# The banks of the latent queries' other products, a later rotation, and row maxima that begin 14 groups behind the gate keys

## The chip, the cores and the metric

The kernel runs on one core of one Trainium2 chip. The metric is the time of one execution on the device in microseconds (us). The kernel before was timed three times; the median stands for it. One further execution was recorded by the hardware profiler, and every row of a profile below comes from that one.

## The reference, cut to what matters

Two layers over a sequence of 1024 tokens with 1024 features. Each layer projects the normalized input once and gives parts of it to three mixers: retention (4 heads), latent attention (8 heads, "mla") and gated linear attention (4 heads, "gla"). Their gated outputs are joined and projected back.

```python
for l in range(DEPTH):                                   # DEPTH = 2
    h = rms_norm(x, norm_w[l]) * (1 + scale) + shift     # scale, shift, gate from c @ ada_w[l]
    ret_p, mla_p, gla_p = split_cols(h @ w_in[l], ...)
    rq, rk, rv, rz = split_cols(ret_p, RET_SPLIT)
    r_o = rms_norm(retention(rope(rq), rope(rk), rv))
    mq, mkv, mkr, mz = split_cols(mla_p, MLA_SPLIT)
    m_o = mla(mq, mkv, mkr, ...)
    gq, gk, gv, gg, gz = split_cols(gla_p, GLA_SPLIT)
    g_o = rms_norm(gla(gq, gk, gv, gg, ...), gla_norm[l])
    x = x + gate * (concat(r_o * silu(rz), m_o * silu(mz), g_o * silu(gz)) @ w_out[l])

def mla(q_lat, kv_lat, k_rope, ...):
    q = rms_norm(q_lat) @ w_uq                # per head 64 plain and 32 rotated columns
    q_nope, q_pe = q[..., :64], rope(q[..., 64:], pos)
    k_nope, v = split(rms_norm(kv_lat) @ w_ukv);  k_pe = rope(k_rope)
    sc = (q_nope . k_nope + q_pe . k_pe) * scale, masked by chunk
    return softmax(sc) @ v
```

## The kernel before, in words

Products are taken in single precision from operands that are split in a high and a low part, so that each product is a group of three matmuls (`mm3`, L556 to L558: high by high, high by low, low by high). TensorE (PE) runs its instructions in the order in which the program writes them. The queues of the other engines, SyncE's (SP) among them, which issues the transfers, are put in order by a scheduler. The accumulators lie in four pools of two banks each: `pj`, `mm`, `s` and `acc`. A product may begin in a bank when the instructions that read the bank's last product are done.

Small pieces of work run beside the large projections. `task(steps, wait)` registers a generator, `tick()` stands behind each group of three matmuls and counts the waits down, a generator's `yield n` puts it off for n groups, and `drain` runs a task out.

The stages of a layer around the change, in the order of TensorE, with their names in the tiles of the profile:

- `mla_queries`, first part: four products of the rotated query columns. They are copied to tiles `mq_qx`, two for each half of the sequence. The first half is rotated there and then (`q_rope`).
- `rz0`: the first half of retention's gate, `proj_silu` (copy from the bank L717, silu in L430 to L435 on ScalarE, VectorE and GpSimd).
- `mla_queries`, the rest: eight products p0 to p7 of the plain query columns (four pairs of heads `pr`, two halves `hf` of the sequence). Each has two groups (0.23 us a matmul), and each is read by ScalarE (cast to the high part `mq_ph`, L1108) and by VectorE (low part `mq_pl`, L1109), and goes to memory (`qn`, L1111). Behind p7 `q_rope` rotates the second half: six products on VectorE (`rope_half`, L732 to L737; the tiles `mrope_ra` and `mrope_rb` hold two of them, the rest is done in place in `mq_qx`), two casts on VectorE (`mrope_qrh`, L1120), two subtractions on GpSimd (`mrope_qrl`, L1121), four transfers to memory (`qr`, L1123).
- `rz1`: the second half of retention's gate, as `rz0`.
- `gk`: the gate keys, 16 groups of three. Beside them run `head_out` (L874 on TensorE, L878 on VectorE: it multiplies retention's output by the gate, then L883 writes it to memory, `md`) and the first row maxima, `mla_max`.
- `gv`, and then the gate stages of the other mixers.

`ret_core` runs beside all of these stages up to the end of `rz1`. Per chunk pair and head group it makes scores (L790), masks them on VectorE (`retc_ram`, L793), takes the state products (L815, states `mq_rst` L825), and sums the output in a bank of `acc` (L830, L834, with `retc_rqs` of GpSimd, L798); ScalarE copies it out (`retc_ho`, L850) and squares it (L860), VectorE sums the squares (`hnorm`, L862), and GpSimd normalizes (L864).

`mla_max` finds the maximum of each row of raw scores before the attention. `load(h)` brings the rows of head h to one of two pairs of tiles: `mmax_mxk` (keys) and `mmax_mxq` (queries: plain rows from `qn` L1149, rotated rows from `qr` L1151, both halves of the sequence at once). Twelve matmuls per head (L1244) each with a maximum on VectorE (L1246) follow, one about every 1.45 groups, and the results are put together behind them (L1213 to L1220). `wgk`, `wgv` and `wgz` are weights: their high part is cast by ScalarE (L456), the low part is subtracted by GpSimd (L457). `ada_aw` (L575 loads, L576 on VectorE) prepares the modulation of layer 1 during layer 0. `glap_wg` (L891) is a small weight read for the decay (matmul L908).

Of the kernel before, what the change touches and what calls it, by code (L numbers as in the profile page):

```python
# [162 lines left out]
class Builder:  # L163
# [903 lines left out]
    def mla_queries(self, l, ql, tab):  # L1067

        nc = self.nc
        w, wn = self.weight((l, "uq"))  # L1070
        self.lab = "mq_"
        x = [[], []]
        for hf in range(2):
            for i in range(2):
                ps = self.ps("pj")
                self.uq_mtile(w, ql, i, hf, ps)
                x[hf].append(self.pt(name="qx"))
                nc.scalar.copy(x[hf][i], ps)
            if hf == 0:
                self.q_rope(l, x[hf], hf, *tab[hf])  # L1080
                self.lab = "mq_"
        yield
        self.lab = "mq_"
        for pr in range(4):
            for hf in range(2):
                ps = self.ps("pj")
                self.uq_mtile(wn, ql, pr, hf, ps)
                self.pair_out(self.qn[l], pr, hf, ps)
        self.q_rope(l, x[1], 1, *tab[1])

    def mla_keys(self, l, kvl):
# [376 lines left out]
    def layer(self, l, src):  # L1468
        nc = self.nc
        self.chunks.extend([(l, 4), (l, 5)] + ([(l + 1, i) for i in (0, 2, 1, 3)] if l + 1 < DEPTH else []))  # L1470
        mixed = [None] * 8
# [30 lines left out]
        queries = self.mla_queries(l, ql, tab)  # L1502
        next(queries)
        mixed[0] = self.proj_silu(l, "rz0")
        self.next_chunk("f")
        next(queries, None)
        mixed[1] = self.proj_silu(l, "rz1")
        self.drain(core)
        self.next_chunk("g")
        big = self.task(self.mla_max(l), 8)  # L1510
        hout = self.task(self.head_out(l, ro, mixed, (0, 1)))
        gk = self.proj_halves(l, "gk", float(GDK ** -0.5))
        self.drain(hout)
# [75 lines left out]
```

## Time and profile before

| what | value |
|---|---|
| median of 3 runs | 1170.69 us (1167.6, 1170.69, 1170.9) |
| the profiled execution | 1170.77 us, its span 1169.0 us |
| mean granted TensorE clock | 0.984 of full speed |
| TensorE busy | 1117.3 us, 96% of the span, 5968 matmuls |
| VectorE busy | 792.6 us, 68% |
| ScalarE busy | 596.0 us, 51% |
| GpSimd busy | 527.0 us, 45% |
| transfers | 169.01 MB, mean 145 GB/s |

The span is what the trace covers; some 1.8 us of the execution lie outside it. Busy shares are means over stages that differ, so what the change is worth is read in the stages that it touches. In a row of a timeline stand the start in us, the duration in us, engine, line, operation, and output<-input; "x2" says that two such instructions in a row are taken together; a bracket gives the idle time of the engine just before and what ended it. Layer 0 passes the stages around the change about 562.7 us earlier than layer 1.

### The profile page before, as it was taken

The numbers are of one execution on the slowest core, as the hardware profiler recorded it, in microseconds if no ns is written. First come the engines' busy times: TensorE is split into PE (matmuls) and PEld (weight loads), VectorE is DVE, ScalarE is ACT, GpSimd is POOL, SyncE is SP. The second block draws the span as 40 slices with busy tenths as digits, with TensorE's granted clock in tenths as the row PEclk, the third lists the DMA queues.
The fourth block names the chain that finished last, engine by engine and source line by source line (L and its number), as shares of the span: only waits on it lengthen the run. The fifth ranks groups of instructions, "written<-read, shape, count | busy, mean of one in ns | idle before, by whom it ended". The sixth has DMA issues, their size and how long they took to land.

```text
span 1169.0 us, 16968 instructions
## 1 busy us (share of the span) xinstructions
PE 1117.3 (96%) x5968; PEld 937.6 (80%) x5968; DVE 792.6 (68%) x1366; ACT 596.0 (51%) x1164; POOL 527.0 (45%) x459
## 2 busy tenths in 40 slices
PE   6999999999999899999999999989999989999996
PEld 4778987788877788887887898778888778888896
DVE  7866585688777366768875467674876735686754
ACT  6434343433544678853543434434355467886421
POOL 0064144444533456773565333534552344668620
PEclk8999999999999999999999999999999989999998
DMA  9816563561146534248443356255212653424722
GB/s 372 298 53 181 186 225 109 188 203 41 42 136 179 132 91 109 64 158 301 171 171 103 111 172 239 77 190 160 64 41 64 178 132 91 109 64 168 255 82 73
DMA packets 65585, 169.01 MB, mean 145 GB/s; under 512 B 10262, under 2 KB 13334, under 8 KB 65500
## 3 DMA queue, kind: packets, MB, share of 16 engines
q1 hardware_dynamic: 65500, 167.93, 45.4%
q8 instruction: 47, 0.77, 0.3%
q14 instruction: 38, 0.31, 0.1%
HBM read 125.36 MB, written 38.41 MB: 140 GB/s over the span
## 4 chain that ended last, share of the span: by engine, by line
PE 74%; DVE 12%; DMA 5%; ACT 4%; issue 4%; POOL 1%; SPq 0%; DVEq 0%; ACTq 0%; POOLq 0%
PE mhead_psacc L1295 3%; PE mhead_psacc L1293 3%; PE mhead_psacc L1294 3%; PE pmz_pspj L556 3%; PE pmz_pspj L557 2%; PE pmz_pspj L558 2%; DMA ada_aw<-awc 2%; PE wo_pspj L558 2%; PE wo_pspj L556 2%; PE wo_pspj L557 2%; PE wo_pss L558 2%; PE wo_pss L556 2%; PE wo_pss L557 2%; PE mhead_pss L1262 2%; PE mhead_pss L1261 2%
## 5 line engine op out<-in xcount | busy, mean ns | idle before, releaser
L457 POOL TENSOR_TENSOR wwo_wl<-wwo_wst,wwo_wh 128x1024 fp32r<-128x1024 f32 x27 | 69.3, 2570 | 40.8 <-ACT wwo_wh L456 33.7
L1270 POOL TENSOR_TENSOR mhead_wh<-mhead_p,mhead_wh 128x384 fp32r<-128x384 f32 (+1 forms) x48 | 58.1, 1210 | 46.2 <-DVE mhead_wh L1269 46.2
L576 DVE SCALAR_TENSOR_TENSOR ada_aw<-ada_aw,silrow 128x512 f32<-128x512 f32 x64 | 60.6, 966 | 20.7 <-DMA ada_aw<-awc 20.7
L1246 DVE TENSOR_REDUCE mmax_mx<-mmax_psmm 128x1 f32<-128x512 f32 (+1 forms) x96 | 57.4, 598 | 25.0 <-PE mmax_psmm L1244 23.5
L1275 DVE TENSOR_TENSOR mhead_ph<-mhead_pss,mhead_ph 128x512 fp32r<-128x512 f32 x48 | 33.0, 688 | 41.9 <-ACT mhead_pss L1274 41.9
L556 PE MATMUL pmz_pspj<-mkh_h,wmz_wh 128*128 128x512 f32 x128 | 53.6, 418 | 0.0
L557 PE MATMUL pmz_pspj<-mkh_h,wmz_wh 128*128 128x512 f32 x128 | 50.9, 397 | 0.0
L558 PE MATMUL pmz_pspj<-mkh_h,wmz_wl 128*128 128x512 f32 x128 | 50.7, 396 | 0.0
L1270 POOL TENSOR_TENSOR mhead_wl<-mhead_p,mhead_wl 128x128 fp32r<-128x128 f32 (+1 forms) x48 | 35.8, 747 | 32.7 <-DVE mhead_wl L1269 32.7
L558 PE MATMUL wo_pspj<-gran_mx,wwo_wl 128*128 128x512 f32 (+1 forms) x120 | 45.1, 375 | 1.9 <-POOL wwo_wl L457 1.9
L556 PE MATMUL wo_pspj<-gran_mx,wwo_wh 128*128 128x512 f32 (+1 forms) x120 | 45.2, 377 | 0.3 <-ACT wwo_wh L456 0.3
L557 PE MATMUL wo_pspj<-gran_mx,wwo_wh 128*128 128x512 f32 (+1 forms) x120 | 44.7, 372 | 0.0
L556 PE MATMUL wo_pss<-gran_mx,wwo_wh 128*128 128x512 f32 (+1 forms) x120 | 44.6, 372 | 0.0
L558 PE MATMUL wo_pss<-gran_mx,wwo_wl 128*128 128x512 f32 (+1 forms) x120 | 44.2, 368 | 0.0
L557 PE MATMUL wo_pss<-gran_mx,wwo_wh 128*128 128x512 f32 (+1 forms) x120 | 44.2, 368 | 0.0
L600 ACT ACTIVATE ssq_sq<-ssq_x 128x512 f32<-128x512 f32 (+1 forms) x31 | 16.6, 534 | 52.0 <-DVE ssq_x L1372 52.0
L457 POOL TENSOR_TENSOR wrk_wl<-wrk_wst,wrk_wh 128x1024 fp32r<-128x1024 f32 x3 | 8.0, 2676 | 75.7 <-ACT wrk_wh L456 75.7
L605 DVE TENSOR_TENSOR ssq_sq<-ssq_sq,ssq_sq 128x512 f32<-128x512 f32 (+1 forms) x30 | 30.0, 999 | 13.9 <-ACT ssq_sq L600 13.9
L1273 ACT ACTIVATE mhead_ph<-mhead_pss 128x512 fp32r<-128x512 f32 x48 | 28.6, 596 | 17.2 <-PE mhead_pss L1263 16.7
L556 PE MATMUL pv_pspj<-wgv_wh,mkh_h 128*128 128x256 f32 x128 | 37.2, 291 | 0.0
L1262 PE MATMUL mhead_pss<-pmz_stkql,pmz_stkkh 96*128 96x512 f32 x96 | 36.6, 381 | 0.0
L1261 PE MATMUL mhead_pss<-pmz_stkqh,pmz_stkkh 105*128 105x512 f32 x96 | 36.6, 381 | 0.0
(565 smaller groups left out, 4121.2 us busy)
## 6 DMA issues: line engine op xcount, KB each, us to landing
ada_aw<-awc SPq DMA_DIRECT2D x64, 256.0 KB
wwo_wst<-wo SPq DMA_DIRECT2D x32, 512.0 KB
aw<-awc SPq DMA_DIRECT2D x11, 512.0 KB
x<-xT SPq DMA_DIRECT2D x8, 512.0 KB
kn<-mk_ph SPq DMA_DIRECT2D x16, 256.0 KB
kn<-mk_pl SPq DMA_DIRECT2D x16, 256.0 KB
qn<-mq_ph SPq DMA_DIRECT2D x16, 256.0 KB
qn<-mq_pl SPq DMA_DIRECT2D x16, 256.0 KB
```

The source lines that it names most:

```text
L457: (eng or nc.gpsimd).tensor_tensor(lo, src, hi.bitcast(F32), ALU.subtract)
L556: mm(ps, lh, rh, start=start, stop=False)
L557: mm(ps, lh, rl, start=False, stop=False)
L558: self.last = mm(ps, ll, rh, start=False, stop=stop)
L576: step = nc.vector.scalar_tensor_tensor(v, v, 1.0, self.silrow[:, cs], ALU.mult, ALU.mult, accum_out=t[:, 2 * j + i:2 * j + i + 1])
L1246: nc.vector.tensor_reduce(mx[:, i, j:j + 1], ps[:, :w], AX.X, ALU.max)
L1261: mm(s, st["kh"][0:105, ks], st["qh"][0:105, qs], start=True, stop=False)
L1262: mm(s, st["kh"][0:96, ks], st["ql"][0:96, qs], start=False, stop=False)
L1270: nc.gpsimd.tensor_tensor(pl, p, ph.bitcast(F32), ALU.subtract)
L1293: mm(acc[:, o], vh, ph, start=(j == 0), stop=False, skip_group_check=True)
L1294: mm(acc[0:64, o], vl, ph, start=False, stop=False, skip_group_check=True)
L1295: mm(acc[:, o], vh, pl, start=False, stop=last, skip_group_check=True)
```

## The change

Three edits, made in both layers.

1. In the second part of `mla_queries` the products p2 and p5 (every third) take a bank of the pool `acc` in place of one of `pj`. The other six still take turns in the two banks of `pj`.
2. A `yield` stands ahead of the second `q_rope`. The layer goes on with the generator only after `rz1` is written, so the rotation of the second half stands behind `rz1` in the program.
3. The task `mla_max` waits for 14 groups of `gk` in place of 8 before its first step (which issues the loads of head 0; the first matmul comes 1.45 groups later).

```diff
         for pr in range(4):
             for hf in range(2):
-                ps = self.ps("pj")
+                ps = self.ps("acc" if (2 * pr + hf) % 3 == 2 else "pj")
                 self.uq_mtile(wn, ql, pr, hf, ps)
                 self.pair_out(self.qn[l], pr, hf, ps)
+        yield
         self.q_rope(l, x[1], 1, *tab[1])
...
         next(queries)
         mixed[0] = self.proj_silu(l, "rz0")
         self.next_chunk("f")
+        next(queries)
+        mixed[1] = self.proj_silu(l, "rz1")
         next(queries, None)
-        mixed[1] = self.proj_silu(l, "rz1")
         self.drain(core)
         self.next_chunk("g")
-        big = self.task(self.mla_max(l), 8)
+        big = self.task(self.mla_max(l), 14)
```

The lines of the kernel after are one higher from L1089 on and two higher from the layer's `next` on. Names keep their numbers below, since rows would read alike without them.

First place: ScalarE's queue in layer 1, at the casts of p0, p1 and p2 (`mq_ph`), beside the normalization of retention's output (L445 to L447 are the steps of its reciprocal root). Before:

```order
L860 ACTIVATE hnorm_hsq_7423<-retc_ho_7361 128x512
L1108 CAST mq_ph_7435<-mq_pspj_7384 128x512
L1108 CAST mq_ph_7448<-mq_pspj_7441 128x512
L445 ACTIVATE hnorm_sm_7426<-hnorm_sm_7425,eps 128x8
L446 ACTIVATE hnorm_sm_7426<-hnorm_sm_7426 128x8
L447 ACTIVATE hnorm_sm_7427<-hnorm_sm_7426 128x8
L1108 CAST mq_ph_7461<-mq_pspj_7454 128x512
L850 COPY retc_ho_7505<-retc_psacc_7498 128x256
```

After:

```order
L860 ACTIVATE hnorm_hsq_7423<-retc_ho_7361 128x512
L1109 CAST mq_ph_7435<-mq_pspj_7384 128x512
L1109 CAST mq_ph_7448<-mq_pspj_7441 128x512
L445 ACTIVATE hnorm_sm_7426<-hnorm_sm_7425,eps 128x8
L446 ACTIVATE hnorm_sm_7426<-hnorm_sm_7426 128x8
L1109 CAST mq_ph_7461<-mq_psacc_7454 128x512
L447 ACTIVATE hnorm_sm_7427<-hnorm_sm_7426 128x8
L850 COPY retc_ho_7505<-retc_psacc_7498 128x256
```

The cast of p2 reads a bank of `acc` and stands one small instruction earlier; the rest of ScalarE's queue in this stage is as it was.

Second place: VectorE's queue in layer 1 around `gk`, from the first `head_out` product (L878) to the first maximum. Before:

```order
L878 TENSOR_TENSOR mq_rz_1539_7232<-hout_psacc_7768,mq_rz_1539_7232 128x512
L878 TENSOR_TENSOR mrope_rz_1633_7629<-hout_psacc_7780,mrope_rz_1633_7629 128x512
L433 SCALAR_TENSOR_TENSOR prz_zu_7747<-mrope_rz_1633_7629,prz_zt_7746 128x512
L878 TENSOR_TENSOR mq_rz_1539_7232<-hout_psacc_7792,mq_rz_1539_7232 128x512
L878 TENSOR_TENSOR mrope_rz_1633_7629<-hout_psacc_7804,mrope_rz_1633_7629 128x512
L1246 TENSOR_REDUCE mmax_mx_7842<-mmax_psmm_7844 128x1
```

After:

```order
L878 TENSOR_TENSOR mq_rz_1627_7609<-hout_psacc_7780,mq_rz_1627_7609 128x512
L433 SCALAR_TENSOR_TENSOR prz_zu_7727<-mq_rz_1627_7609,prz_zt_7726 128x512
L732 TENSOR_TENSOR mrope_ra_7734<-mq_qx_7230,pv_tab_6923 128x512
L733 TENSOR_TENSOR mrope_rb_7735<-mq_qx_7190,pv_tab_6923 128x512
L878 TENSOR_TENSOR mq_rz_1539_7232<-hout_psacc_7792,mq_rz_1539_7232 128x512
L736 TENSOR_TENSOR mq_qx_7230<-mq_qx_7230,pv_tab_6922 128x512
L734 TENSOR_TENSOR mq_qx_7190<-mq_qx_7190,pv_tab_6922 128x512
L878 TENSOR_TENSOR mq_rz_1627_7609<-hout_psacc_7804,mq_rz_1627_7609 128x512
L737 TENSOR_TENSOR mq_qx_7230<-mq_qx_7230,mrope_rb_7735 128x512
L735 TENSOR_TENSOR mq_qx_7190<-mq_qx_7190,mrope_ra_7734 128x512
L1121 CAST mrope_qrh_7742<-mq_qx_7190 128x512
L1121 CAST mrope_qrh_7748<-mq_qx_7230 128x512
```

The eight rows of the rotation, which stood ahead of `rz1`'s silu and of retention's last `retc_ram`, now stand behind the last silu step of `rz1` (L433), among the last two products of `head_out`. In layer 0 six rows L576 (`ada_aw`) stand between the last cast and the first maximum.

Third place: SyncE's queue in layer 1, where the rotated rows go to memory (`qr`) and come back for the maxima (`mmax_mxq<-qr`). Before:

```order
L1123 DMA qr_101<-mrope_qrh_7617 128x512
L1123 DMA qr_101<-mrope_qrh_7623 128x512
L1123 DMA qr_101<-mrope_qrl_7618 128x512
L1123 DMA qr_101<-mrope_qrl_7624 128x512
L1202 DMA mmax_mxk_7814<-mrows 8x1024
...
L1149 DMA mmax_mxq_7813<-qn_109 64x1024
L1151 DMA mmax_mxq_7813<-qr_101 16x1024 x2
L1153 DMA mmax_mxk_7814<-kn_111 64x1024
```

After:

```order
L883 DMA md_105<-mq_rz_1539_7232 128x1024
L883 DMA md_105<-mq_rz_1627_7609 128x1024
L1124 DMA qr_101<-mrope_qrh_7742 128x512
L1124 DMA qr_101<-mrope_qrh_7748 128x512
L1124 DMA qr_101<-mrope_qrl_7743 128x512
L891 DMA glap_wg_1682_7885<-wg 128x128
L1152 DMA mmax_mxq_7836<-qr_101 16x1024
L1124 DMA qr_101<-mrope_qrl_7749 128x512
L1152 DMA mmax_mxq_7836<-qr_101 16x1024
```

The other loads of the first two heads (masks, keys, plain queries) now stand ahead of these rows. The rotated rows are written behind `head_out`'s result, and read back behind GpSimd's low parts. In layer 0 three loads of `ada_aw` stand among these rows. On TensorE the first maximum (`mmax_psmm<-mmax_mxk,mmax_mxq`) stood behind the 30th of the 48 matmuls of `gk`; it now stands behind the 48th, ahead of the first matmul of `gv`. The last ones end 12 matmuls later, in the last stage before the attention.

## The prediction

> **What bounds the kernel now.** I read the page first, for the engine that carries the chain, then TensorE's own waits, for what the three edits can win.
>
> ```profile
> span 1169.0 us, 16968 instructions
> PE 1117.3 (96%) x5968; PEld 937.6 (80%) x5968; DVE 792.6 (68%) x1366; ACT 596.0 (51%) x1164; POOL 527.0 (45%) x459
> ...
> PE 74%; DVE 12%; DMA 5%; ACT 4%; issue 4%; POOL 1%; SPq 0%; DVEq 0%; ACTq 0%; POOLq 0%
> ```
>
> TensorE is busy for 96% of the span. The number of matmuls does not change, so only its idle time can be won or added: 51.7 us over the whole span. Its waits by releaser (total, times, longest):
>
> ```profile
> PE mv_pspj L556 <- DVE pmz_vl L1191: 7.2, 2, 3.6
> ...
> PE mq_pspj L556 <- DVE mq_pl L1109: 3.7, 4, 1.6
> ...
> PE prz_pspj L556 <- DVE mq_pl L1109: 2.4, 2, 1.2
> ...
> PE glap_psacc L908 <- DMA glap_wg<-wg: 1.1, 1, 1.1
> ...
> PE retc_psacc L830 <- DVE retc_ram L793: 0.8, 2, 0.5
> PE retc_psacc L834 <- POOL retc_rqs L798: 0.7, 2, 0.4
> ```
>
> The second row is what the bank edit aims at, the third the first product of `rz1` behind the queries, the last two the end of retention inside `rz1`. Everything within reach adds up to 8 us. None of these rows names the maxima's loads: their rows of today arrive before they are wanted. That margin is what edits two and three spend.
>
> **Edit one, the banks.** Timeline of TensorE, then ScalarE and VectorE, at p1/p2 and at the end of the pairs in layer 1:
>
> ```profile
> 759.47 0.40 PE L558 MATMUL mq_pspj<-latn_lat,wuq_wl 128*128 128x512 f32 x1
> 761.42 0.50 PE L556 MATMUL mq_pspj<-latn_lat,wuq_wh 128*128 128x512 f32 x1 [1.56 <-DVE mq_pl L1109]
> ...
> 777.36 0.51 PE L556 MATMUL prz_pspj<-mkh_h,wrz_wh 128*128 128x512 f32 x1 [1.22 <-DVE mq_pl L1109]
> ...
> 774.78 0.37 ACT L850 COPY retc_ho<-retc_psacc 128x256 f32<-128x256 f32 x1 [3.59 <-PE retc_psacc L834]
> 775.24 0.63 ACT L860 ACTIVATE hnorm_hsq<-retc_ho 128x512 f32<-128x512 f32 x1
> 775.77 1.05 ACT L1108 CAST mq_ph<-mq_pspj 128x512 fp32r<-128x512 f32 x2
> ```
>
> p2 waits until VectorE has read p0's bank. With a bank of `acc` it need not: 1.56 us are gone, and the smaller wait of p5 with it (the four waits are 3.7, so 1.85 a layer). p3, which now wants p0's bank, comes 1.5 us after p2 and finds it nearly free; I set what it still waits against the slow restarts that vanish. The banks of `acc` also serve retention's outputs, but those are copied by ScalarE's L850 ahead of the cast in the same queue, so no product of retention waits for p2 or p5 longer than it does now: cost nothing, and up to 0.4 us a layer if that cover fails (one L850). The wait at 777.36 stays: p6 and p7 still use `pj`, and their casts stand behind L850 and L860, which no edit moves. **−3.7 us** in both layers, bounds −2 (p3 takes over half) and −4.5.
>
> **Edit two, what it wins.** The end of retention in `rz1`, layer 1, and the same step undisturbed among the pairs:
>
> ```profile
> 756.96 1.00 PE L830 MATMUL retc_psacc<-pv_v,retc_ram 128*128 128x64 f32 x8
> ...
> 758.22 0.48 PE L556 MATMUL mq_pspj<-latn_lat,wuq_wh 128*128 128x512 f32 x1
> ...
> 786.72 0.39 PE L558 MATMUL prz_pspj<-mkh_h,wrz_wl 128*128 128x512 f32 x1
> 787.37 1.12 PE L830 MATMUL retc_psacc<-pv_v,retc_ram 128*128 128x64 f32 x8 [0.25 <-DVE retc_ram L793]
> ...
> 789.74 0.48 PE L556 MATMUL prz_pspj<-mkh_h,wrz_wh 128*128 128x512 f32 x1
> ...
> 778.42 2.88 DVE L733 TENSOR_TENSOR mrope_rb<-mq_qx,pv_tab 128x512 f32<-128x512 f32 x1
> 782.51 0.68 DVE L737 TENSOR_TENSOR mq_qx<-mq_qx,mrope_rb 128x512 f32<-128x512 f32 x1
> 785.40 1.36 DVE L1120 CAST mrope_qrh<-mq_qx 128x512 fp32r<-128x512 f32 x1
> 786.79 0.76 DVE L793 TENSOR_TENSOR retc_ram<-retc_pss,cst 128x256 f32<-128x256 f32 x2
> 788.13 1.31 POOL L798 TENSOR_TENSOR retc_rqs<-prk_rh,cst 128x128 f32<-128x128 f32 x2
> ```
>
> L793 and L798 came late because the rotation stood ahead of them on VectorE and its low parts on GpSimd. From the last product to the next it took 3.02 us (786.72 to 789.74); undisturbed 0.23 and 1.26 (756.96 to 758.22). The difference, 1.5 us, is won in each layer: **−3.0 us**, bounds −1.5 (the two waits alone) and −3.4.
>
> **Edits two and three, what they cost.** In `gk`, layer 1: VectorE, GpSimd, the first matmul of `gk` and the first of `gv`, and the transfers' latencies among the queries:
>
> ```profile
> 793.94 0.39 PE L556 MATMUL pgk_pspj<-mkh_h,wgk_wh 128*128 128x512 f32 x1
> 802.64 0.23 PE L1244 MATMUL mmax_psmm<-mmax_mxk,mmax_mxq 104*128 104x128 f32 x1
> ...
> 807.67 0.28 PE L556 MATMUL pv_pspj<-wgv_wh,mkh_h 128*128 128x256 f32 x1
> ...
> 797.16 0.69 DVE L878 TENSOR_TENSOR mrope_rz<-hout_psacc,mrope_rz 128x512 f32<-128x512 f32 x1 [1.21 <-PE hout_psacc L874]
> 798.51 2.54 DVE L433 SCALAR_TENSOR_TENSOR prz_zu<-mrope_rz,prz_zt 128x512 f32<-128x512 f32 x1 [0.65 <-ACT prz_zt L432]
> ...
> 795.75 4.76 POOL L457 TENSOR_TENSOR wgv_wl<-wgv_wst,wgv_wh 128x1024 fp32r<-128x1024 f32 x2 [1.32 <-ACT wgv_wh L456]
> 801.86 1.29 POOL L435 TENSOR_TENSOR mrope_rz<-mrope_rz,prz_zu 128x512 f32<-128x512 f32 x1 [1.35 <-ACT prz_zu L434]
> ...
> 768.89 0.32 SPq L1111 DMA_DIRECT2D qn<-mq_pl  x1
> ...
> 771.07 0.88 POOL L798 TENSOR_TENSOR retc_rqs<-prk_rh,cst 128x128 f32<-128x128 f32 x2 [6.82 <-DMA qn<-mq_pl]
> ...
> 791.31 1.04 SPq L1151 DMA_DIRECT2D mmax_mxq<-qr  x2
> ```
>
> I count from `gk`'s first matmul, t0 = 793.94. When the rows are wanted: `gk` takes 13.73 us with five maxima in it, which cost from start to start 0.06 to 0.24, together 0.8. The first maximum now stands behind all of `gk`: t0 + 12.9 (before, t0 + 8.7 at 802.64).
>
> When they arrive: VectorE's L433 stands ahead of the rotation and ends at t0 + 7.1; it can't begin sooner, since it follows the silu steps of `rz1`'s last product. Then come six rotation rows and two L878, each 0.60 from start to start (a row of 0.68 as at 782.51, less the overlap): t0 + 11.9. Two casts of 0.48 make it t0 + 12.8. GpSimd's two low parts (1.29, the length of the L435 row) follow the casts: t0 + 13.6 and 14.9. SyncE's queue holds the low parts' writes ahead of the last read back, so that read is issued at about t0 + 15.9 (0.3 for a write, 0.52 for a read: 1.04 for two). A write of this kind took 2.2 us from issue to the instruction that waited (768.89 to 771.07); I take as much for the read, whose own time no row shows: t0 + 18.2. In layer 1 TensorE then stands still for **5.3 us**. The least is 2.3: the high parts' writes land 2.2 after the casts (t0 + 15.0), nothing is held up by the low parts, and the read back takes next to nothing. The most is 7: VectorE's rows are held by GpSimd's (L433 took 2.54 beside the weight's split, L733 2.88, a cast 1.36) once more than counted.
>
> Here a rule bears. The Trainium skill ("SBUF — State Buffer", section "SBUF: two separate sides") says that VectorE with two operands in SBUF and GpSimd share a pair of ports under an exclusive lock, and whichever comes second is blocked for the other's whole instruction. The trace agrees (beside the same weight split L433 took 2.54 us, and L878, with an operand in PSUM, 0.69). By it L435 and the low parts each hold a row of the rotation, some 1.3 us more, and the stall would be 6.6.
>
> In layer 0 the same chain holds, and the six `ada_aw` rows stand on VectorE ahead of the first maximum; three of their loads stand in SyncE's queue ahead of the read back and may each wait for a buffer that such a row frees (0.60 each): +1.7, so **7.0 us**, bounds 2.3 and 9. What it absorbs: the wait of 1.1 us for `glap_wg` in layer 0, whose load now lands during the stall: **−1.1 us**, bounds 0 and −1.1.
>
> Then the clock. After a long wait TensorE runs slowly. Windows just after the two waits of 3.6 us, of `gk`, and after a short wait (us, busy, then the granted clock in the third column from the end):
>
> ```profile
> 398.25:402.00 3.75, 3.75 (x17) 3.61 (x18) 1.40 (x3) 1.23 (x3) 3.75 (x9) 0.62 0.99 228
> 955.44:961.20 5.76, 5.76 (x24) 5.47 (x24) 2.25 (x4) 2.67 (x5) 3.82 (x9) 0.53 0.73 164
> 793.94:808.00 14.06, 14.06 (x73) 11.71 (x72) 7.13 (x10) 5.75 (x9) 7.69 (x8) 1.00 0.79 224
> 761.42:765.00 3.58, 3.58 (x20) 2.70 (x20) 1.48 (x4) 0.63 (x2) 1.88 (x3) 1.00 0.74 287
> ```
>
> Waits of 3.6 us cost a further 1.4 and 2.7 us (3.75 × 0.38, 5.76 × 0.47); the wait of 1.56 cost none. Stalls of 5 and 7 us should cost the mean of the two each: **+4.0 us**, bounds 0 (both short) and +6. The Trainium skill ("TensorE: Matmul & The Clock Gate", section "What's actually happening") gives half rate after at least one idle window of about 3.4 us; the rows agree. By its rule a stall of less than that costs its length only, as the second rival below has it.
>
> The sum against the profiled 1170.8 us (span and 1.8 around it; the median is 0.1 lower): −3.7 − 3.0 − 1.1 + 5.3 + 7.0 + 4.0 = +8.5, which makes 1179.2 on the median. GpSimd and ScalarE are late by nothing else: the weight split `wgz` that follows on GpSimd is wanted after `gv`. The maxima end 12 matmuls later (2.7 us), still ahead of the attention.
>
> **Rivals.**
> - The rows arrive in time. For it: today they are issued early enough not to be seen at all. Against it: L433's end alone, eight rows and a transfer out and in (7.1 + 4.8 + 4.4 = 16.3) pass 12.9. It decides if the chain falls under 12.9. Time: 1170.7 − 7.8 = 1162.9, and up to 1165 with a stall of 1 a layer. This is the side of faster.
> - A short stall, about 3 us in each layer, under the length after which the clock falls: −7.8 + 6.0 = −1.8, 1168.9; at 4 us, 1170.9. For it: the read of the high parts needs no low part, only the queue's order puts it behind. Against it: that order.
> - A longer stall: the lock holds more rows, and `ada_aw`'s loads hold SyncE in layer 0: 7 and 9 us, clock +6: −7.8 + 16 + 6 = +14, 1185.
> - The bank edit does nothing, p3 and p4 taking over p2's wait: the forecast plus 3.7, 1183.
>
> **How the numbers follow.** The forecast's own form (both stalls of 4.5 to 8 us and a fall of the clock) has a chance of 0.55, with 1175 to 1183 of its own; the longer stall 0.1, the bank edit's failing 0.05; the short stall 0.16; rows in time 0.14. About 0.3% (3.5 us) is what a measurement of this kernel can tell from no change, so slower than 1174.2 is 0.70, within 0.3% is 0.16, faster 0.14. The range runs from 1168.5, with the short stall in it, to 1185; rows in time and the far end of the longer stall are left out.
>
> **What the profile after would show.** Right: no wait of `mq_pspj` at p2 and p5; L830 and L834 of `rz1` without waits and L793 before 780; VectorE's L732 behind L433; a wait of TensorE at the first L1245 (the maximum) for `mmax_mxq<-qr`, 5 us in layer 1 and more in layer 0, a granted clock of about half behind it, and no wait at `glap_wg`. Wrong: no wait at L1245, or one under 3 us; waits of `mq_pspj` at p3 or of `retc_psacc` for a bank; maxima that end behind the last gate product, with VectorE's reduces late.

## The result, and the profile after

The changed kernel took 1179.42 us (median of 4 runs, 1178.73 to 1179.75), against 1170.8 us for the kernel before on the same chip. The ratio is 1.0076, with a 95% interval from 1.0054 to 1.0099. The forecast was 1179.2. The total came out, but both stalls were longer than forecast, and a gain that stands against them was in no term; the experiments say why.

The page after, its span, busy times and waits of TensorE by releaser (total, times, longest). These rows answer to those of before:

```profile
span 1176.9 us, 16987 instructions
PE 1117.0 (95%) x5968; PEld 938.1 (80%) x5968; DVE 795.6 (68%) x1366; ACT 595.3 (51%) x1164; POOL 527.0 (45%) x459
...
PE mmax_psmm L1245 <- DMA ada_aw<-awc: 11.5, 1, 11.5
...
PE mmax_psmm L1245 <- issue: 6.4, 1, 6.4
...
PE prz_pspj L556 <- DVE mq_pl L1110: 2.3, 2, 1.2
...
PE mq_pspj L556 <- DVE mq_pl L1110: 0.4, 2, 0.2
```

TensorE does the same work in the same busy time. The waits at p2 and p5 fell from 3.7 to 0.4 us, those of L830, L834 and `glap_wg` are no longer in the list, and two new rows, one a layer, hold 17.9 us at the first row maximum. Neither releaser is the full cause: 11.5 us are put down to a transfer of `ada_aw`, 6.4 to "issue". The timeline names it. Layer 1, from the end of `rz1` on: TensorE, VectorE, GpSimd, SyncE.

```profile
795.73 0.39 PE L556 MATMUL pgk_pspj<-mkh_h,wgk_wh 128*128 128x512 f32 x1
...
808.29 0.39 PE L558 MATMUL pgk_pspj<-mkh_h,wgk_wl 128*128 128x512 f32 x1
815.07 0.45 PE L1245 MATMUL mmax_psmm<-mmax_mxk,mmax_mxq 104*128 104x128 f32 x1 [6.39 <-issue]
...
800.30 2.54 DVE L433 SCALAR_TENSOR_TENSOR prz_zu<-mq_rz,prz_zt 128x512 f32<-128x512 f32 x1 [0.66 <-ACT prz_zt L432]
...
804.58 1.18 DVE L736 TENSOR_TENSOR mq_qx<-mq_qx,pv_tab 128x512 f32<-128x512 f32 x1
...
803.59 1.61 POOL L435 TENSOR_TENSOR mq_rz<-mq_rz,prz_zu 128x512 f32<-128x512 f32 x1 [1.29 <-ACT prz_zu L434]
...
808.19 0.76 DVE L1121 CAST mrope_qrh<-mq_qx 128x512 fp32r<-128x512 f32 x2
...
808.70 2.60 POOL L1122 TENSOR_TENSOR mrope_qrl<-mq_qx,mrope_qrh 128x512 fp32r<-128x512 f32 x2 [3.49 <-DVE mrope_qrh L1121]
...
808.65 0.80 SPq L1124 DMA_DIRECT2D qr<-mrope_qrh  x2
810.11 0.32 SPq L1124 DMA_DIRECT2D qr<-mrope_qrl  x1
810.53 0.37 SPq L891 DMA_DIRECT2D glap_wg<-wg  x1
811.00 0.41 SPq L1152 DMA_DIRECT2D mmax_mxq<-qr  x1
811.49 0.37 SPq L1124 DMA_DIRECT2D qr<-mrope_qrl  x1
811.96 1.30 SPq L1152 DMA_DIRECT2D mmax_mxq<-qr  x3
```

`gk` begins at t0 = 795.73. L433 ends at t0 + 7.1, the casts at t0 + 13.2 (forecast 12.8), head 0's last read back is issued at t0 + 16.2 (forecast 15.9; the other two reads at 811.96 are head 1's), the maximum begins at t0 + 19.3 (forecast 18.2). TensorE was done with `gk` at t0 + 12.8. The missing 1.1 us is mostly the read itself: from issue to use it took 3.1 us (811.96 to 815.07), where the forecast had taken the 2.2 us of a write. The issue time is near, but not for the forecast's reason. By the semaphore times in the trace, the last high part's write, issued at 809.06, had wholly landed at 811.87, 2.8 us later, and the read went out 0.1 us behind that.

Layer 0 at the same place: SyncE, VectorE, GpSimd, TensorE.

```profile
242.79 3.08 SPq L575 DMA_DIRECT2D ada_aw<-awc  x2
245.97 0.38 SPq L1124 DMA_DIRECT2D qr<-mrope_qrl  x1
246.44 0.85 SPq L1152 DMA_DIRECT2D mmax_mxq<-qr  x2
...
239.33 1.76 DVE L576 SCALAR_TENSOR_TENSOR ada_aw<-ada_aw,silrow 128x512 f32<-128x512 f32 x1
...
241.02 1.74 DVE L576 SCALAR_TENSOR_TENSOR ada_aw<-ada_aw,silrow 128x512 f32<-128x512 f32 x1
...
242.69 2.81 DVE L576 SCALAR_TENSOR_TENSOR ada_aw<-ada_aw,silrow 128x512 f32<-128x512 f32 x1
...
245.44 0.68 DVE L576 SCALAR_TENSOR_TENSOR ada_aw<-ada_aw,silrow 128x512 f32<-128x512 f32 x1
...
239.16 3.05 POOL L1122 TENSOR_TENSOR mrope_qrl<-mq_qx,mrope_qrh 128x512 fp32r<-128x512 f32 x2 [3.50 <-DVE mrope_qrh L1121]
242.17 2.78 POOL L457 TENSOR_TENSOR wgz_wl<-wgz_wst,wgz_wh 128x1024 fp32r<-128x1024 f32 x1
244.90 1.33 POOL L897 MEMSET glap_gka<- 64x256 f32 x4
...
250.61 0.44 PE L1245 MATMUL mmax_psmm<-mmax_mxk,mmax_mxq 104*128 104x128 f32 x1 [11.47 <-DMA ada_aw<-awc]
```

Three loads of `ada_aw` stand ahead of the read back; the last two, shown together in the first row, hold SyncE until 245.9. Each waits for a buffer that a row L576 frees, and these rows took 1.76, 1.74 and 2.81 us here, not 0.60, beside GpSimd's low parts and a weight split.

Behind both waits the clock is low (windows: us, busy, then the granted clock third from the end):

```profile
250.61:256.00 5.39, 5.39 (x28) 5.39 (x29) 2.82 (x9) 0.00 (x0) 0.00 (x0) 0.59 0.88 297
815.07:820.00 4.93, 4.93 (x28) 4.92 (x29) 1.27 (x3) 0.00 (x1) 0.00 (x0) 0.68 0.36 110
```

That is 2.2 and 1.6 us (5.39 × 0.41, 4.93 × 0.32).

To compare kernels stage by stage I take, from TensorE's timelines, the time from a stage's first matmul to the next one's. In layer 1, us:

| stage | before | after | banks alone | banks, start 14, early rotation | rotation in rz1, start 14 |
|---|---|---|---|---|---|
| p0 to rz1 | 23.22 | 21.27 | 21.26 | 21.21 | 21.21 |
| rz1 to gk | 16.58 | 15.00 | 16.57 | 16.58 | 15.00 |
| gk to gv | 13.73 | 19.58 | 13.73 | 12.85 | 12.85 |
| gv to gz | 31.48 | 33.08 | 31.47 | 31.80 | 31.81 |
| gz to mz | 51.35 | 50.15 | 51.40 | 50.10 | 50.13 |
| mz to the attention's values | 59.52 | 60.35 | 59.52 | 60.36 | 60.36 |

The stages that a kernel leaves alone agree within 0.1 us here. Over the whole execution they do not agree so well: stretches at a low clock come and go. One window of 10 us in layer 0, ahead of anything that the change touches, before and after (granted clock third from the end):

```profile
175.00:185.00 10.00, 8.65 (x45) 7.28 (x43) 5.38 (x17) 2.91 (x8) 4.26 (x6) 0.83 0.49 158
```

```profile
175.00:185.00 10.00, 8.66 (x57) 7.02 (x55) 6.02 (x21) 4.16 (x10) 4.57 (x7) 1.00 0.52 160
```

The kernel before lost 1.7 us there (10 × 0.17) and the changed one nothing. Such a difference between two executions is no effect of the change: from `rz0` to the queries that follow it, where this window lies, layer 0 takes 20.0 us in the profiled executions of six of this document's thirteen kernels and 18.4 to 18.5 in the other seven, with the kernel before in the first group and the same kernel with the bank edit alone, which does not touch this stage, in the second.

### The profile page after: what moved, and what is told of

Same layout as the page of the kernel before. It is cut to its first block, busy times and chain, and to the rows that moved or that the text cites. A ratio compares the mean times of both kernels' runs of the same rounds, so it can differ in the third digit from the quotient of the medians.

```text
span 1176.9 us, 16987 instructions
## 1 busy us (share of the span) xinstructions
PE 1117.0 (95%) x5968; PEld 938.1 (80%) x5968; DVE 795.6 (68%) x1366; ACT 595.3 (51%) x1164; POOL 527.0 (45%) x459
## 4 chain that ended last, share of the span: by engine, by line
PE 68%; DVE 13%; issue 6%; DMA 4%; ACT 4%; POOL 4%; SPq 0%; DVEq 0%; POOLq 0%; ACTq 0%
PE mhead_psacc L1296 3%; PE mhead_psacc L1294 3%; PE mhead_psacc L1295 3%; PE pmz_pspj L556 2%; PE pmz_pspj L557 2%; PE pmz_pspj L558 2%; PE mhead_pss L1262 2%; PE mhead_pss L1263 2%; PE mhead_pss L1264 2%; DVE mmax_mx L1247 2%; DVE ada_aw L576 2%; PE pgz_pspj L556 1%; PE pv_pspj L556 1%; PE wo_pss L558 1%; PE wo_pss L557 1%
## 5 line engine op out<-in xcount | busy, mean ns | idle before, releaser
L576 DVE SCALAR_TENSOR_TENSOR ada_aw<-ada_aw,silrow 128x512 f32<-128x512 f32 x64 | 61.9, 985 | 19.1 <-DMA ada_aw<-awc 18.9
L1245 PE MATMUL mmax_psmm<-mmax_mxk,mmax_mxq 104*128 104x512 f32 (+1 forms) x96 | 35.3, 367 | 19.9 <-DMA ada_aw<-awc 11.5
L600 ACT ACTIVATE ssq_sq<-ssq_x 128x512 f32<-128x512 f32 (+1 forms) x31 | 16.5, 533 | 53.1 <-DVE ssq_x L1373 53.1
L1245 PEld LDWEIGHTS mmax_psmm<-mmax_mxk,mmax_mxq 104*128 104x128 f32 x96 | 18.3, 191 | 25.0 <-issue 18.6
```

What stands on the lines that cost most here:

```text
L576: step = nc.vector.scalar_tensor_tensor(v, v, 1.0, self.silrow[:, cs], ALU.mult, ALU.mult, accum_out=t[:, 2 * j + i:2 * j + i + 1])
L1245: nc.tensor.matmul(ps[:, :w], st["q"][0:104, 128 * i:128 * i + 128], st["k"][0:104, 512 * j:512 * j + w], start=True, stop=True)
```

## Experiments

My theory was that both early gains are real and add up, and that the loss is the rotated rows' arrival alone. The rivals were that late maxima cost by themselves, and that the moved rotation gets in the way of other work in `gk`. The first four kernels take the edits apart.

**The banks alone.** Kernel before with edit one.

```diff
-                ps = self.ps("pj")
+                ps = self.ps("acc" if (2 * pr + hf) % 3 == 2 else "pj")
```

> The bank edit alone (rotation ahead of rz1, maxima from group 8). If the bank edit wins what the changed kernel's trace shows between the first product of the pairs and rz1 (2.0 us a layer), about 1166.8 against 1170.8 before. If p3 and p4 only take over p2's wait, 1170 to 1171. Waits of mq_pspj should fall from 3.7 to about 0.4 us, the waits in rz1 (L830, L834) stay.

Measured: 1168.31 us, ratio 0.998 (0.996 to 1.0001), runs from 1162.4 to 1172.6. The stage from p0 to `rz1` is 1.96 us shorter in layer 1 and 2.03 in layer 0 (23.24 to 21.21), so the mechanism is shown; the execution's time is too scattered to show 4 us. In the profiled one, the slowest of the ten, layer 0 lost them again: 1.6 us in `rz1`, where the granted clock was 0.91, and 5.4 from `gv` to `gz`, in these two waits and behind them (0.52 from 252.8 to 258.0):

```profile
250.43 0.39 PE L1244 MATMUL mmax_pss<-mmax_mxk,mmax_mxq 104*128 104x256 f32 x1 [1.77 <-DVE mmax_mx L1246]
252.86 1.85 PE L908 MATMUL glap_psacc<-turn_pt,glap_wg 48*128 48x512 f32 x2 [1.33 <-DMA glap_wg<-wg]
```

**Edits one and three, the rotation early.**

```diff
-        yield
...
-        next(queries)
-        mixed[1] = self.proj_silu(l, "rz1")
         next(queries, None)
+        mixed[1] = self.proj_silu(l, "rz1")
```

> Edits one and three without edit two: the rotation stays ahead of rz1, the maxima begin 14 groups behind. If the loss comes from the rotated rows alone, there is no wait at the first maximum, rz1 keeps its 1.5 us a layer, and the time is 1165.5 to 1167. If late maxima are themselves what costs (their work moved into the gate values' stage, or their end ahead of the attention), 1171 or more.

Measured: 1162.95 us, ratio 0.9954 (0.9934 to 0.9974). No wait at the first maximum, so the loss needs the later rotation. It is also 2.6 us below the lowest figure that I expected. The table shows a gain that was in no term: from `gk` to the attention layer 1 takes 155.11 us instead of 156.08. Layer 0 gains more. From `gz` to the attention it takes 114.9 to 115.0 us with a start at 8 (before, banks alone, and the rotation in `rz1` with start 8 below), and 112.6 (to 0.1) with a start at 14 (this kernel, the changed one and four others). The stage from `mz` on, before and after:

```profile
329.25:392.83 63.58, 61.40 (x279) 48.71 (x278) 42.35 (x90) 31.61 (x59) 21.76 (x19) 0.97 0.58 167
```

```profile
334.62:397.06 62.44, 60.85 (x284) 48.12 (x282) 46.02 (x94) 31.59 (x59) 22.18 (x20) 1.00 0.66 182
```

TensorE waits less there, and the clock does not fall. Over both layers TensorE's waits for VectorE's maxima and their closing fall from 6.1 to 3.7 us in this kernel and in the changed one. Those in the decay core (`glac`, L971, 1.6 us) are gone, and the longest, in the closing (L1217, 1.5 us), is 1.1.

**Edits one and two, start 8.**

```diff
-        big = self.task(self.mla_max(l), 14)
+        big = self.task(self.mla_max(l), 8)
```

> Edits one and two without edit three: rotation behind rz1, maxima from group 8. If the rows set the time, they arrive when they did (19.3 us behind the first matmul of gk in layer 1, 24.4 in layer 0) but are wanted 4.2 us sooner: waits of about 10.6 and 15.7 us at the first maximum, 1187 to 1188. If late maxima cost, the time falls back to 1171 or less.

Measured: 1192.34 us, ratio 1.02 (1.0165 to 1.0234). Waits of TensorE:

```profile
PE mmax_psmm L1245 <- DMA mmax_mxq<-qr: 25.1, 2, 14.3
```

The waits are 10.8 and 14.3 us, and their sum 7.2 above the 17.9 of the changed kernel. The releaser is now the read back itself. The rows set the time, and the later start softens the loss rather than causing it. That excludes the first rival. The time is 4 us above what I expected; 3.7 of it stand in layer 0 from `gz` to the attention (116.3 us against the changed kernel's 112.6), where the later start had won.

**The rotation inside rz1.** VectorE stands idle for 5.4 us there once the rotation is gone (791.75, wait of 5.43 ahead of L433 in the changed kernel); the rotation is put in that gap, behind retention's last rows.

```diff
         next(queries)
+        rot = self.task(queries, 6)
         mixed[1] = self.proj_silu(l, "rz1")
-        next(queries, None)
+        self.drain(rot)
```

> The changed kernel with one more edit: the rotation is registered as a task that begins 6 groups into rz1, so that on VectorE it stands behind retention's last L793 and L825 and ahead of rz1's silu. If the place of the rotation is the whole cause, VectorE does it in the 5.4 us it stands idle there, both gains stay and no wait is left at the first maximum: 1162 to 1163.5. If contention or the late maxima cost too, 1166 or more.

Measured: 1166.07 us, ratio 0.9959 (0.9943 to 0.9976), and no wait for rows. Layer 1 is the sum of all gains (last column of the table), which leaves nothing to the second rival there. The time is 3 to 4 us above what I expected, and layer 0 shows why:

```profile
249.86 1.60 PE L908 MATMUL glap_psacc<-turn_pt,glap_wg 48*128 48x512 f32 x2 [4.18 <-DMA glap_wg<-wg]
...
246.63 0.38 SPq L891 DMA_DIRECT2D glap_wg<-wg  x1
```

The load of `glap_wg` stands behind `ada_aw` in SyncE's queue. The sooner TensorE gets there, the longer it waits; the clock falls behind it, and layer 0 takes 39.07 us from `gv` to `gz` (32.63 before).

**Why layer 0 waits longer than layer 1.** The changed kernel with the `ada_aw` chunk of that place moved behind `gv`.

```diff
-CHUNKS = "ccgkno"
+CHUNKS = "ccikno"
```

> The changed kernel with the loads and sums of ada_aw that stand in layer 0 between the rotation and the first maximum moved behind the gate values' stage. If they are why layer 0 waits 11.5 us where layer 1 waits 6.4, layer 0's wait falls to 6 to 7 us and the time by about 5, to 1174 to 1175. If layer 0 waits longer for another reason (its other transfers), the wait stays above 9 us and the time at 1177 or more. Layer 1 has no such rows and should not change.

Measured: 1181.39 us, ratio 1.0076 (1.0054 to 1.0098). Half of this came as expected, both layers now wait for the same 6.38 us:

```profile
248.77 0.44 PE L1245 MATMUL mmax_psmm<-mmax_mxk,mmax_mxq 104*128 104x128 f32 x1 [6.38 <-issue]
...
819.18 0.45 PE L1245 MATMUL mmax_psmm<-mmax_mxk,mmax_mxq 104*128 104x128 f32 x1 [6.38 <-issue]
...
298.86 0.70 PE L996 MATMUL glac_psmm<-pv_v,glac_gks 128*128 128x256 f32 x2 [0.95 <-DVE mmax_mx L1247]
300.53 0.48 PE L971 MATMUL glac_psmm<-cst,glap_gkl 128*128 128x128 f32 x1 [0.97 <-DVE mmax_mx L1247]
```

So the 5.1 us by which layer 0 waited longer are `ada_aw`'s. The time did not fall, since the sums now hold VectorE in the gate stage of layer 0: `gz` to `mz` takes 56.46 us there in place of 50.11. The cost moved.

**A much later start.** The changed kernel with a start at 32 groups.

```diff
-        big = self.task(self.mla_max(l), 14)
+        big = self.task(self.mla_max(l), 32)
```

> The changed kernel with maxima that begin 32 groups behind the first of gk, so 16 groups of the gate values (0.36 us each, 5.8 us) later than in the change; the rotation stays behind rz1. If the rows' arrival is the loss, layer 1's wait falls from 6.4 to under 1 us and layer 0's from 11.5 to 5 to 6, with less lost to the clock: 1165 to 1168. If late maxima cost by themselves (they now end some 50 matmuls later), 1172 or more.

Measured: 1188.72 us, ratio 1.0137 (1.0116 to 1.0159). This missed by over 20 us. No matmul waits for rows any more, but:

```profile
252.93 2.04 PE L908 MATMUL glap_psacc<-turn_pt,glap_wg 48*128 48x512 f32 x2 [7.09 <-DMA glap_wg<-wg]
...
280.26 0.79 PE L1245 MATMUL mmax_psmm<-mmax_mxk,mmax_mxq 104*128 104x512 f32 x1 [7.48 <-DVE mmax_mx L1247]
...
279.04 0.84 DVE L935 TENSOR_TENSOR glap_gka<-pgk_gk,glap_gt 64x256 f32<-64x256 f32 x2
279.91 0.29 DVE L1247 TENSOR_REDUCE mmax_mx<-mmax_psmm 128x1 f32<-128x128 f32 x1
```

`glap_wg` stands behind the rotated rows' writes and is no longer hidden by a stall (7.1 and 2.4 us), and VectorE's queue puts the first maxima behind the whole decay chain of both halves (L913 to L935), so the fifth maximum waits 7.5 us for a bank in each layer. The rows were one of three things that had to be on time.

**The rotation inside rz1, chunk moved.** Both edits of above in one kernel.

> The kernel with the rotation inside rz1 (6 groups in), and the ada_aw loads moved behind the gate values as well. If the wait of 4.2 us for glap_wg that layer 0 had there comes from those loads standing ahead of it in SyncE's queue, it is gone, with the slow clock behind it: 1160 to 1162. If the moved loads only put the wait elsewhere (the gate stage), 1165 or more.

Measured: 1163.82 us, ratio 0.993 (0.9913 to 0.9948). The wait for `glap_wg` is gone, layer 0's `gv` takes 31.81 us, and 4.8 of the 7.3 us won come back in the gate stage (50.13 to 54.90), by the same collision.

**The rotation inside rz1, start 8.**

```diff
-        big = self.task(self.mla_max(l), 14)
+        big = self.task(self.mla_max(l), 8)
```

> The kernel with the rotation inside rz1, and maxima that begin 8 groups behind as before the change. The rows come about 4 us ahead of need or a little late by then. If a start at 14 saves about 1 us a layer by itself (the sum of the stages from the queries to the attention in layer 1 was 0.96 shorter where the rows were on time), 1167 to 1169 against 1166.1 with 14. If the start is worth nothing where no rows are late, 1165.5 to 1166.5.

Measured: 1166.56 us, ratio 0.9964 (0.9946 to 0.9982). By the times alone the start is worth nothing here that can be told. By the stages of layer 1, `gk` to the attention takes 156.14 us against 155.15 with a start at 14: 1.0 us, the same as in the early rotation. In layer 0 it takes 167.14 against 164.50, though the wait for `glap_wg` is 1.7 us here and 4.2 there. The two profiled executions are equally long all the same, since the one with a start at 14 is 3.6 us longer outside these stages. So what the start is worth in the whole time is not shown by this pair.

**glap_wg first.** Its load is issued ahead of `ada_aw`; once with the rotation inside `rz1`, once with it early.

```diff
+        self.lab = "glap_"
+        self.wg2 = self.pt((128, 128), name="wg2")
+        nc.sync.dma_start(self.wg2, self.A["wg2"][l])
         self.next_chunk("g")
...
-        wg = self.pt((128, 128), name="wg2")
-        nc.sync.dma_start(wg, self.A["wg2"][l])
+        wg = self.wg2
```

> The kernel with the rotation 6 groups into rz1 and maxima from group 14, and the load of glap_wg issued ahead of layer 0's ada_aw loads (they stay where they were). If the wait of 4.2 us for glap_wg and the slow clock behind it (2 to 3) are all that was left of the change's loss, 1159 to 1161. If the ada_aw sums hold up something else in the gate values' stage once that wait is gone, 1162 to 1165.

> Edits one and three with the rotation ahead of rz1 as before the change, and the load of glap_wg issued ahead of ada_aw: 1.9 us of waiting less than the 1162.95 without it, 1160.5 to 1162. Against the same with the rotation inside rz1 it shows what retention's late end in rz1 costs: 3.1 us more if the two stages (16.58 against 15.0 us in both layers) are all that differs; within 1 us if the one is given back elsewhere.

Measured: 1161.95 us, ratio 0.9906 (0.9887 to 0.9924), with the rotation inside `rz1`; 1161.34 us, ratio 0.9898 (0.9883 to 0.9912), with it early. Both beat the kernel before and the changed one by about 1% and 1.5%, and both have no wait for `glap_wg`. They are equal within what can be told, though `rz1` is 1.6 us shorter in each layer of the first (15.0 against 16.6 us). In its layer 0 1.9 us go again from `gv` to `gz` (34.12 against 32.24), where a maximum waits for VectorE:

```profile
264.77 0.44 PE L1244 MATMUL mmax_psmm<-mmax_mxk,mmax_mxq 104*128 104x384 f32 x1 [1.22 <-DVE mmax_mx L1246]
```

Besides, its profiled execution is 1.2 us longer in each of two stretches (up to layer 0's `rz1`, and from layer 0's attention to layer 1's `rz1`) in which the two kernels do the same work. Whether those are chance, and so which of the two is the better, stays open.

**The low parts on another queue.** The changed kernel with the writes of the second half's `mrope_qrl` issued from ScalarE's queue.

```diff
-                nc.sync.dma_start(self.qr[l][i, j, :, hs], t.bitcast(F32))
+                (nc.scalar if j and hf else nc.sync).dma_start(self.qr[l][i, j, :, hs], t.bitcast(F32))
```

> The changed kernel with the writes of the second half's low parts issued from ScalarE's queue in place of SyncE's, so that the rows' read back stands behind no low part. If the low parts ahead of it in the queue hold the read (the prediction counted about 0.9 us), the waits at the first maximum fall by 0.5 to 1 us in each layer, 1178 to 1179. If the landing of the high parts' writes holds it, the waits stay at 6.4 and 11.5.

Measured: 1179.23 us, ratio 1.0052 (1.0032 to 1.0072), two runs. Layer 1 still waits, layer 0 0.9 us less:

```profile
814.38 0.45 PE L1245 MATMUL mmax_psmm<-mmax_mxk,mmax_mxq 104*128 104x128 f32 x1 [6.52 <-issue]
...
807.82 0.80 SPq L1124 DMA_DIRECT2D qr<-mrope_qrh  x2
...
809.91 0.32 SPq L1152 DMA_DIRECT2D mmax_mxq<-qr  x1
...
811.37 1.26 SPq L1152 DMA_DIRECT2D mmax_mxq<-qr  x3
...
SPq L1152 <- DMA qr<-mrope_qrh: 1.8, 2, 1.1
...
251.77 0.45 PE L1245 MATMUL mmax_psmm<-mmax_mxk,mmax_mxq 104*128 104x128 f32 x1 [10.54 <-DMA mmax_mxq<-qr]
```

In layer 1 the first read goes out at t0 + 15.0 instead of t0 + 15.3 (t0 = 794.91), the second at t0 + 16.5 instead of 16.2, and the maximum begins at t0 + 19.5 where it was 19.3. The row of SyncE's own waits names what holds the reads: 1.8 us in two waits, both for the high parts' writes to land. So the write out and back holds the rows there, not the low parts ahead of them; in layer 0 the low parts hold a little.

## Why the prediction was right, point by point

- *The bank edit, −3.7 us.* Right: −4.0 (−1.95 and −2.03). p3 waits 0.2 us, as forecast, and no product waits for a bank of `acc`. The wait of 1.2 at `rz1` stayed.
- *Retention's end in `rz1`, −3.0 us.* Right: −3.4 (−1.58 and −1.82). Undone by putting the rotation back, kept by putting it behind L793.
- *The wait at the first maximum, 5.3 us in layer 1.* Right in place and within its bounds, 6.4 in size; the chain from VectorE through memory is right, its last link is not. The prediction let the low parts ahead of the read in SyncE's queue set its issue (t0 + 15.9). They held it by nothing that shows in layer 1: the read waited for the high parts' writes, 2.8 us where 2.2 was taken. That t0 + 16.2 is so near is chance. The read then took 3.1 us where 2.2 was taken, and collisions with GpSimd 0.4 (L736 took 1.18 beside L435). The 6.6 that the prediction gives by the lock rule is near 6.4 for another reason too: it has 1.3 us of blocked rows, and one row lost 0.5.
- *The same in layer 0, 7.0 us.* Mis-sized: 11.5, beyond its upper bound of 9. The +1.7 for `ada_aw` was really 5.1. It was counted as three rows of 0.60; they took 1.74 to 2.81 beside GpSimd. Moving the chunk showed that the whole 5.1 is its.
- *The clock, +4.0 us.* Right: 3.8.
- *`glap_wg`, −1.1 us.* Right, and larger than it looked: without the stall that hides it the wait grows to 4.2 (rotation inside `rz1`) or 7.1 (start at 32).
- *The later maxima, nothing.* Wrong: −1.0 us in layer 1 and about −2.9 in layer 0 (`gk` 0.9 and `gz` to the attention 2.4 shorter, `gv` 0.3 longer as in layer 1), where TensorE waits less for maxima and a fall of the clock in the stage from `mz` on does not come.
- *The sum.* +8.5 was forecast, the spans differ by 7.9 and the medians by 8.6. Stalls 5.6 us too low stand against the later maxima (about 3.9), gains 0.7 better, a clock 0.2 better, and 1.4 us in stages that the change does not touch, where the two profiled executions differ by their stretches of low clock. That the median came out within 1 us is chance: two errors of 4 to 6 us of opposite sign. The sign, and that the stalls outweigh the gains, are not.

## What to carry to other kernels

Before work is moved later on an engine, follow its result to the next reader, through every queue and transfer on the way, and compare that arrival with the moment of need; here a round trip through memory alone used 6 us of a margin of 13. If there is an idle gap on the same engine between the work that was delayed and the reader, that gap is a place to try: behind retention's rows, the rotation kept both gains. In the whole time, though, leaving it early did as well (1161.34 us against 1161.95). And when a stall goes, look for what it hid: the small load of `glap_wg` behind the larger `ada_aw` loads was late each time TensorE got there sooner, until one of the two was moved.

## What the runs showed of the hardware that was not expected

A read of 16 rows from memory that had just been written took 3.1 us from issue to use (811.96 to 815.07), and the write that it followed 2.8 us from issue to landing, against the 2.2 us of an earlier write in the kernel before.

VectorE's sums over two operands in SBUF (L576), 0.68 us alone, took 1.74 to 2.81 us beside GpSimd's subtractions, so work that is queued in a stretch of GpSimd work costs up to four times its length; the Trainium skill ("SBUF — State Buffer", section "SBUF: two separate sides") gives the exclusive lock of the shared ports as the reason, and these rows agree with it. Beside GpSimd's memset at 244.90, which reads nothing, such a sum took its 0.68 us.

The prediction's rows show the clock falling behind waits of 3.6 us and not behind one of 1.56. A shorter wait can stand ahead of a low clock all the same, and not in every execution. In layer 0, before and after:

```profile
177.16 1.01 PE L790 MATMUL retc_pss<-prk_rh,prk_rh 64*128 64x128 f32 x8 [1.35 <-DVE retc_ram L793]
```

```profile
177.31 1.01 PE L790 MATMUL retc_pss<-prk_rh,prk_rh 64*128 64x128 f32 x8 [1.34 <-DVE retc_ram L793]
```

The granted clock from 175 to 185 was 0.83 in the kernel before and 1.00 in the changed one. What decides between the two is not shown.
